# Operand steps of the down-projection issued behind named weight splits, operand sums on VectorE, and linear attention's products with v first

## The chip, the cores and the metric

One core of a Trainium2 chip runs the whole kernel. The metric is the device time in microseconds. Engines are named as in the profile: PE is TensorE (matmuls) and PEld its weight loads, DVE is VectorE, ACT is ScalarE, POOL is GpSimd, SP is SyncE, whose queue issues nearly all DMAs.

## What is computed

One decoder layer on 512 tokens of width 2048, in float32: an input projection, three groups of heads (windowed softmax attention, gated linear attention, stick-breaking attention), an output projection with a residual, and a squared-ReLU MLP with a residual, then a last RMSNorm.

```python
x = x + token_mixing(rmsnorm(x, norm_mix), w_in, ...)        # three head groups, then @ w_out
h = rmsnorm(x, norm_mlp)
x = x + jnp.square(jax.nn.relu(h @ w_mlp_in)) @ w_mlp_out     # 2048 -> 8192 -> 2048
out = rmsnorm(x, norm_final)

# inside token_mixing, linear attention in chunks of 64 tokens:
o = einsum(scores, v) + einsum(q_dec, s_prev)                 # products with v, products with the state
```

## The kernel before

**Products.** Every float32 matrix product is made of three matmuls on rounded halves: each operand x is split into hi (ScalarE rounds it to float32r) and lo (VectorE subtracts hi from x), and hi·hi, hi·lo and lo·hi are added in PSUM. The large products also use Strassen's scheme: `strassen` (L222) makes seven products A11, S1, S2, A12, S3, S4, A22 in place of eight. Their weight operands come from `t_operands` (L182): for each product it splits two halves of 128x1024 (`whi` on ScalarE at L200, `wlo` on VectorE at L201, three buffers each) and, behind the splits of each of the first four products, makes two differences of weights on VectorE (`diff`, L174).

**The up-projection** (from L1266) goes through 16 blocks b of 512 hidden columns. A block has 7 products of 2 halves of 24 matmuls each. Its results are added up and squared (`after`, `finish`) into the tiles `av`. Two blocks make one group g of 1024 columns, so there are 8 groups.

**The down-projection's operands.** Its Strassen operands (A11, A12, A22 and the sums S1 to S4 of the squared activations) are made while the up-projection runs. `down_half` (L1231) is called when a half of a block is finished. It calls `down_split` (L1223), which makes dh on ScalarE (L1226) and dl on VectorE (L1227) and issues two DMAs of 512 KB to DRAM (the tensors dS). Where S1, S2, S4 and A22 are concerned it puts closures into `later_steps`; `next_step` takes one out after each following product. dh and dl share a pool tag with two buffers, so a step that needs both waits until the two DMAs of the one before have read them.

**The down-projection** (from L1363) runs `row_group` (L944) for the 8 groups. It reads those operands back from DRAM and w_mlp_out as weights.

**Sums on GpSimd.** `mixed_operands` makes four sums of the attention output for the output projection with GpSimd in its first use (`G if k1`), and `s2_op` and `s4_op` make four sums for the first up-projection block through the table `ENG`, all on GpSimd. They are eight tensor operations of 128x1024 (L174 and L171 on POOL).

**Linear attention.** `gl_values` (L734) handles 128 tokens and four heads. For each of two pairs of heads it takes a PSUM bank and per head multiplies the scores with v (L770) and then the decayed queries with the state of each chunk (L775).

**Order.** The program is written in one order; a scheduler then orders the instructions of each engine by priority (`tc.high_priority` for weights and their splits) and by its own estimate of when they are ready. An engine's queue is in order on the chip: an instruction that waits holds all that stand behind it.

Of the kernel before, what the change touches and what calls it, by code (L numbers as in the profile page):

```python
# [10 lines left out]
F32 = mybir.dt.float32  # L11
# [4 lines left out]
ALU = mybir.AluOpType  # L16
AX = mybir.AxisListType

P = 128
# [44 lines left out]
def trunk(ctx, tc, x, norm_mix, w_in, sinks, rel_bias, gate_w, gate_b, gla_norm,  # L64
# [113 lines left out]
    ORDER0 = ("A11", "A12", "S1", "S2", "S4", "S3", "A22")  # L178

    def t_operands(quad, order, ahead=True, before=None):  # L180

# [10 lines left out]
        for p in order:  # L192
            if before:
                before(p)
            with tc.high_priority() if ahead else nullcontext():
                res = []
                for half in src[p]:
                    hi = wp.tile(shape, F32R, tag="whi", name="whi", bufs=3)
                    lo = wp.tile(shape, F32R, tag="wlo", name="wlo", bufs=3)
                    S.activation(hi, half, AF.Copy)  # L200
                    V.tensor_tensor(out=lo, in0=half, in1=hi.bitcast(F32), op=ALU.subtract)  # L201
                    res.append((hi, lo))
# [18 lines left out]

    def strassen(quad, sops, mm, nb, after, order=ORDER, before=None, by_rows=False, ahead=True):  # L222
# [511 lines left out]
    def gl_values(st, t):  # L734
# [27 lines left out]
        ssb = sm.tile([P, GLA_H], F32, tag="ssb", name="ssb")  # L762
        ob = []
        for pr, vt in enumerate(st["bv"]):
            o = pz.tile([P, 512], F32, tag="z", name="oB")
            for u in range(2):
                h = 2 * pr + u
                us = slice(u * DV, (u + 1) * DV)
                hv = slice(h * DV, (h + 1) * DV)
                T.matmul(o[:, us], lhsT=sc[:, h * P : (h + 1) * P], rhs=vt[:, us], start=(u == 0), stop=False,  # L770
                         skip_group_check=True)
                for c in range(2):
                    if prev[c] is not None:
                        cs = slice(c * 64, c * 64 + 64)
                        T.matmul(o[cs, us], lhsT=qdT[:DK, h * P + c * 64 : h * P + c * 64 + 64], rhs=prev[c][:, hv],  # L775
                                 start=False, stop=(u == 1 and c == 1), skip_group_check=True)
            for u in range(2):
                h = 2 * pr + u
# [164 lines left out]

    def row_group(acc, sops, wsrc, k1, k2, done=None, order=ORDER, rscale=None, before=None, spare=None):  # L944
        for np_ in range(2):
# [16 lines left out]
            def after(p, X, Y, Z, rows):  # L962
# [3 lines left out]
                for u in rows:  # L966
# [10 lines left out]
            strassen(quad, sops, mm, 2, after, order, None if np_ else before, by_rows=done and np_)  # L977

# [56 lines left out]
    def mixed_operands(k1, k2, tile_=lambda n: tp4.tile([P, 2, 512], F32, tag="t", name=n), spare=None):  # L1035
# [15 lines left out]

        steps = s_operands(a, put, lambda: [(spare or tile_)("spare")], (G if k1 else V,))

# [95 lines left out]

    ENG = ((G, G), (G, G))  # L1150
    STEPS = {
# [71 lines left out]
    def down_split(g, p, t, last=False):  # L1223
# [5 lines left out]
        nc.sync.dma_start(dS[g][p][1], lo.bitcast(F32))  # L1229

    def down_half(b, th):  # L1231

        g, j = divmod(b, 2)
        a = quads
        if (j, th) == (0, 0):
            down_split(g, "A11", a[1, 1])
        elif (j, th) == (0, 1):
            sub(a[1, 1], a[1, 1], a[2, 1], V)
            down_split(g, "S3", a[1, 1])
        elif (j, th) == (1, 0):  # L1240
            down_split(g, "A12", a[1, 2])
        else:
            q = dict(a)

            def s1_step():
                add(q[2, 1], q[2, 1], q[2, 2], V)
                down_split(g, "S1", q[2, 1], True)

            def s2_step():
                sub(q[1, 1], q[2, 2], q[1, 1], V)  # L1250
                down_split(g, "S2", q[1, 1])

            def s4_step():
                sub(q[1, 2], q[1, 2], q[1, 1], V)
                down_split(g, "S4", q[1, 2], True)


            later_steps.extend([lambda: down_split(g, "A22", q[2, 2]), s1_step, s2_step, s4_step])

    later_steps = []  # L1260

    def next_step():
        if later_steps:
            later_steps.pop(0)()

    for b in range(DFF // 512):  # L1266
# [44 lines left out]

        strassen(wquad, up_ops, mm, 1, after, *((ORDER0, up_operand) if b == 0 else ()), ahead=b > 0)

# [48 lines left out]
    for g in range(NG):  # L1362
# [3 lines left out]
        if g == NG - 1:  # L1366
            pool = places.pop(0)
            for nh in range(2):
                gt = slot(pool[nh], "gfin", (P, 1024))
                nc.sync.dma_start(gt, bcast(norm_final[nh * 1024 : (nh + 1) * 1024], 1024))  # L1370
                gfin.append(gt)
        row_group(acc, sops, w2, g * 1024, g * 1024 + 512,
                  *((y_done, ORDER0) if g == NG - 1 else (None, ORDER)), rscale=r2, spare=next_step)

# [32 lines left out]
```

## Time and profile before

| | us |
|---|---|
| median of 3 runs | 2130.52 (2130.04 to 2140.49) |
| the profiled execution, its own time | 2129.26 |
| its span, first to last instruction | 2127.5 |
| PE busy | 2050.9 (96%) |
| DVE busy | 1665.9 (78%) |
| ACT busy | 1038.6 (49%) |
| POOL busy | 97.8 (5%) |

The stages by the trace's clock: projections and attention up to about 690 us (linear attention about 425 to 545, windowed attention about 545 to 690, beside it the first half of the output projection), the second half of the output projection to about 800, the up-projection to about 1480, the down-projection to the end. A busy PE is not idle in the trace, but it may run at half clock: PEclk is the granted share of 2.4 GHz. A duration of one matmul overlaps that of the next; what a stretch costs PE is read from the starts.

### The profile page before, as it was taken

What the parts mean: (1) busy time and instruction counts of PE and PEld (TensorE: products, weight loads), DVE (VectorE), ACT (ScalarE), POOL (GpSimd) and SP (SyncE); (2) the same over time, 40 slices, a digit from 0 to 9 for tenths busy, and PEclk for the clock granted to TensorE, in tenths of its full rate; (3) what the DMA queues carried; (4) which work ended last, traced back from release to release, by engine and by line L of the source; (5) the groups of instructions that cost most, each with busy time, mean ns of one, the idle gap of its engine ahead of it and who ended that gap; (6) DMA issues with size and microseconds to landing.
All of it is one profiled execution on the core that took longest, in us unless ns stands there. A gap on an engine that the chain in (4) does not pass through costs nothing. (4 is left out here: it accounts for less than half of the span.)

```text
span 2127.5 us, 30668 instructions
## 1 busy us (share of the span) xinstructions
PE 2050.9 (96%) x12174; PEld 1778.3 (84%) x12174; DVE 1665.9 (78%) x1936; ACT 1038.6 (49%) x1500; POOL 97.8 (5%) x63
## 2 busy tenths in 40 slices
PE   8999999999888997999999999999999999999997
PEld 7998888777777777999999999999788888888876
DVE  7876654435787988788788788887998988888887
ACT  6436654323464555565555565564433333333334
POOL 1110000011200002000000000000000000000012
PEclk9999999999999999999999999999999999999999
DMA  6375333425534351555554464469766466455532
GB/s 221 121 159 160 118 128 109 141 98 156 192 107 155 112 175 44 181 203 187 188 216 182 167 231 179 179 235 375 259 220 236 159 215 221 178 197 218 187 130 79
DMA packets 180906, 373.17 MB, mean 175 GB/s; under 512 B 19800, under 2 KB 44186, under 8 KB 180762
## 3 DMA queue, kind: packets, MB, share of 16 engines
q1 hardware_dynamic: 180762, 371.20, 50.2%
q8 instruction: 96, 1.57, 0.3%
q14 instruction: 48, 0.39, 0.1%
HBM read 287.01 MB, written 84.15 MB: 174 GB/s over the span
## 5 line engine op out<-in xcount | busy, mean ns | idle before, releaser
L200 ACT ACTIVATE whi<-raw 128x1024 fp32r<-128x1024 f32 x532 | 561.5, 1059 | 680.9 <-PE X L960 239.0
L201 DVE TENSOR_TENSOR wlo<-raw,whi 128x1024 fp32r<-128x1024 f32 x532 | 647.8, 1229 | 150.8 <-ACT whi L200 149.2
L174 DVE TENSOR_TENSOR raw<-raw 128x1024 f32<-128x1024 f32 x304 | 370.3, 1233 | 31.3 <-DMA raw<-in_w_mlp_in 23.7
L1280 PE MATMUL X<-sh,wlo 128*128 128x256 f32 x1024 | 291.5, 285 | 11.2 <-DVE wlo L201 11.2
L1278 PE MATMUL X<-sh,whi 128*128 128x256 f32 x1024 | 290.8, 284 | 11.0 <-ACT whi L200 10.1
L1279 PE MATMUL X<-sl,whi 128*128 128x256 f32 x1024 | 289.3, 283 | 0.0
L959 PE MATMUL X<-wlo,sh 128*128 128x512 f32 x640 | 256.1, 400 | 2.9 <-DVE wlo L201 2.7
L960 PE MATMUL X<-whi,sl 128*128 128x512 f32 x640 | 254.9, 398 | 0.0
L958 PE MATMUL X<-whi,sh 128*128 128x512 f32 x640 | 232.4, 400 | 12.4 <-ACT whi L200 4.7
L1280 PEld LDWEIGHTS X<-sh,wlo 128*128 128x128 f32 x1024 | 196.3, 192 | 14.4 <-DVE wlo L201 14.4
L1278 PEld LDWEIGHTS X<-sh,whi 128*128 128x128 f32 x1024 | 196.5, 192 | 13.3 <-ACT whi L200 12.1
L1279 PEld LDWEIGHTS X<-sl,whi 128*128 128x128 f32 x1024 | 196.5, 192 | 0.0
L958 PEld LDWEIGHTS X<-whi,sh 128*128 128x128 f32 x640 | 120.5, 189 | 43.7 <-issue 6.2
L959 PEld LDWEIGHTS X<-wlo,sh 128*128 128x128 f32 x640 | 121.4, 190 | 33.9 <-DVE wlo L201 5.8
L1279 PE MATMUL Z<-sl,whi 128*128 128x256 f32 x512 | 143.3, 280 | 2.3 <-DVE sl L1108 2.3
L960 PEld LDWEIGHTS X<-whi,sl 128*128 128x128 f32 x640 | 121.3, 189 | 28.4
L1278 PE MATMUL Z<-sh,whi 128*128 128x256 f32 x512 | 143.4, 280 | 0.1
L1280 PE MATMUL Z<-sh,wlo 128*128 128x256 f32 x512 | 143.1, 280 | 0.0
L959 PE MATMUL Z<-wlo,sh 128*128 128x512 f32 x320 | 127.0, 397 | 0.5 <-DVE wlo L201 0.3
L960 PE MATMUL Z<-whi,sl 128*128 128x512 f32 x320 | 126.6, 396 | 0.0
L958 PE MATMUL Z<-whi,sh 128*128 128x512 f32 x320 | 115.3, 397 | 2.2 <-DVE acc L969 1.1
L113 DVE TENSOR_TENSOR wlo<-raw,whi 128x1024 fp32r<-128x1024 f32 x64 | 80.8, 1267 | 40.3 <-ACT whi L112 38.5
(345 smaller groups left out, 4006.1 us busy)
## 6 DMA issues: line engine op xcount, KB each, us to landing
raw<-in_w_mlp_in SPq DMA_DIRECT2D x64, 1024.0 KB, 6.0
raw<-in_w_mlp_out SPq DMA_DIRECT2D x64, 1024.0 KB, 5.9
raw<-in_w_in SPq DMA_DIRECT2D x28, 1024.0 KB, 5.0
raw<-in_w_out SPq DMA_DIRECT2D x16, 1024.0 KB, 5.2
raw<-in_w_in SPq DMA_DIRECT2D x8, 768.0 KB, 4.8
xt<-in_x SPq DMA_DIRECT2D x16, 256.0 KB, 7.4
raw<-in_w_in SPq DMA_DIRECT2D x8, 512.0 KB, 8.5
raw<-daqk SPq DMA_DIRECT2D x32, 128.0 KB, 2.7
```

Source lines behind the costliest of these rows:

```text
L113: V.tensor_tensor(out=lo, in0=part, in1=hi.bitcast(F32), op=ALU.subtract)
L174: eng.tensor_tensor(out=out_, in0=a, in1=b, op=ALU.subtract)
L200: S.activation(hi, half, AF.Copy)
L201: V.tensor_tensor(out=lo, in0=half, in1=hi.bitcast(F32), op=ALU.subtract)
L958: T.matmul(dst[u], lhsT=sh[:, kc, us], rhs=wh[:, k], start=start and k == 0, stop=False, skip_group_check=True)
L959: T.matmul(dst[u], lhsT=sh[:, kc, us], rhs=wl[:, k], start=False, stop=False, skip_group_check=True)
L960: T.matmul(dst[u], lhsT=sl[:, kc, us], rhs=wh[:, k], start=False, stop=h == 1 and k == 1, skip_group_check=True)
L1278: T.matmul(o, lhsT=wh[:, k, js], rhs=sh[:, k], start=start and j == 0 and k == 0, stop=False, skip_group_check=True)
L1279: T.matmul(o, lhsT=wh[:, k, js], rhs=sl[:, k], start=False, stop=False, skip_group_check=True)
L1280: T.matmul(o, lhsT=wl[:, k, js], rhs=sh[:, k], start=False, stop=h == 1 and k == 3, skip_group_check=True)
```

## The change

1. `later_steps` and `next_step` go. `down_half` puts every step under a key (block, product index), and `strassen` gets a function `beside`, which is called after the weight splits of each product are written and runs the steps of that key. Inside `tc.issue_after(split[0])` and `tc.issue_after(split[1])` each instruction of such a step on ScalarE is ordered behind the last `whi` split, and each on VectorE behind the last `wlo` split, of that product. These edges are an order of issue; they add no wait between engines.
2. Which step stands where changes. Product indices count from 0 in A11, S1, S2, A12, S3, S4, A22. S3 goes to index 4 of the group's second block. A22 goes to index 3, the sums S1 and S2 to index 4 and S4 to index 5 of the next block. The splits of S1 and S2 go to indices 5 and 6 of the block after that (of the next block, in the last group but one). A11 and A12 stay where they were.
3. The eight operand sums on GpSimd go to VectorE (`ENG`, `mixed_operands`).
4. In `gl_values` both PSUM banks are taken at once, all products with v come first, then those with the states, then the squares and copies.

```diff
+    split = [None, None]
@@ t_operands
-                    S.activation(hi, half, AF.Copy)
-                    V.tensor_tensor(out=lo, in0=half, in1=hi.bitcast(F32), op=ALU.subtract)
+                    split[:] = (S.activation(hi, half, AF.Copy).ins,
+                                V.tensor_tensor(out=lo, in0=half, in1=hi.bitcast(F32), op=ALU.subtract).ins)
@@ strassen
         for p, wt in t_operands(quad, order, ahead, before):
+            if beside:
+                with tc.issue_after(split[0]), tc.issue_after(split[1]):
+                    beside(order.index(p))
@@ gl_values
+        os = [pz.tile([P, 512], F32, tag="z", name="oB") for _ in range(2)]
         for pr, vt in enumerate(st["bv"]):
-            o = pz.tile([P, 512], F32, tag="z", name="oB")
+            for u in range(2):
+                h = 2 * pr + u
+                us = slice(u * DV, (u + 1) * DV)
+                T.matmul(os[pr][:, us], lhsT=sc[:, h * P : (h + 1) * P], rhs=vt[:, us], start=(u == 0), stop=False,
+                         skip_group_check=True)
+        for pr, o in enumerate(os):
             for u in range(2):
...
-                T.matmul(o[:, us], lhsT=sc[:, h * P : (h + 1) * P], rhs=vt[:, us], start=(u == 0), stop=False,
-                         skip_group_check=True)
@@ row_group, mixed_operands, table
-                if spare:
-                    spare()
-        steps = s_operands(a, put, lambda: [(spare or tile_)("spare")], (G if k1 else V,))
+        steps = s_operands(a, put, lambda: [(spare or tile_)("spare")], (V,))
-    ENG = ((G, G), (G, G))
+    ENG = ((V, V), (V, V))
@@ down_half
+        def s3():
+            sub(q[1, 1], q[1, 1], q[2, 1], V)
+            down_split(g, "S3", q[1, 1])
+        def s12():
+            add(q[2, 1], q[2, 1], q[2, 2], V)
+            sub(q[1, 1], q[2, 2], q[1, 1], V)
+        def s4():
+            sub(q[1, 2], q[1, 2], q[1, 1], V)
+            down_split(g, "S4", q[1, 2], True)
...
-            later_steps.extend([lambda: down_split(g, "A22", q[2, 2]), s1_step, s2_step, s4_step])
+            at(b + 1, 3, lambda: down_split(g, "A22", q[2, 2]))
+            at(b + 1, 4, s12)
+            at(b + 1, 5, s4)
+            then = b + 1 if g == NG - 2 else b + 2
+            at(then, 5, lambda: down_split(g, "S1", q[2, 1], True))
+            at(then, 6, lambda: down_split(g, "S2", q[1, 1]))
+    def steps_of(block):
+        def beside(i):
+            for f in steps.pop((block, i), ()):
+                f()
+        return beside
@@ up-projection, after
-            if p != "A11":
-                next_step()
```

In the rows of the order below, a name's number tells one tile from another of the same name.

VectorE where the third group ends (block 5) and block 6 begins (raw_9898 to raw_9904 are the next block's weights, av_9008, av_9009, av_9473 and av_9474 the activations of the group that ended), before:

```order
L1227 TENSOR_TENSOR dl_9835<-av_9473,dh_9834 128x1024
L201 TENSOR_TENSOR wlo_9913<-raw_9900,whi_9912 128x1024
L201 TENSOR_TENSOR wlo_9969<-raw_9898,whi_9968 128x1024
L171 TENSOR_TENSOR av_9009<-av_9009,av_9474 128x1024
L174 TENSOR_TENSOR av_9008<-av_9474,av_9008 128x1024
L174 TENSOR_TENSOR raw_9898<-raw_9902,raw_9898 128x4x256
L1227 TENSOR_TENSOR dl_10028<-av_9474,dh_10027 128x1024
L201 TENSOR_TENSOR wlo_9973<-raw_9900,whi_9972 128x1024
L174 TENSOR_TENSOR av_9473<-av_9473,av_9008 128x1024
L174 TENSOR_TENSOR raw_9898<-raw_9898 128x4x256
L201 TENSOR_TENSOR wlo_10035<-raw_9898,whi_10034 128x1024
L1227 TENSOR_TENSOR av_9009<-av_9009,dh_10093 128x1024
```

The same place after, from the same weight split on (the group's second block is now av_9455 and av_9456; av_8110 is a tile of the group before):

```order
L204 TENSOR_TENSOR wlo_9913<-raw_9900,whi_9912 128x1024
L1237 TENSOR_TENSOR dl_9829<-av_9455,dh_9828 128x1024
L204 TENSOR_TENSOR wlo_9969<-raw_9898,whi_9968 128x1024
L174 TENSOR_TENSOR raw_9898<-raw_9902,raw_9898 128x4x256
L174 TENSOR_TENSOR raw_9898<-raw_9898 128x4x256
L204 TENSOR_TENSOR wlo_9973<-raw_9900,whi_9972 128x1024
L1237 TENSOR_TENSOR dl_9843<-av_8110,dh_9842 128x1024
L174 TENSOR_TENSOR raw_9900<-raw_9904,raw_9900 128x4x256
L204 TENSOR_TENSOR wlo_10029<-raw_9898,whi_10028 128x1024
L174 TENSOR_TENSOR raw_9900<-raw_9900 128x4x256
L204 TENSOR_TENSOR wlo_10033<-raw_9900,whi_10032 128x1024
```

Of the operations on activations (av, dl) three stood between the splits wlo_9969 and wlo_9973 and three more up to the end of the piece; now one dl stands ahead of wlo_9969 and one, of the group before, behind wlo_9973; the sums come only thirteen rows behind that split.

SyncE's queue at the same place (dS are the DRAM tensors of the operands), before:

```order
L1228 DMA dS2S30_7102<-dh_9459 128x1024
L1229 DMA dS2S31_7103<-dl_9460 128x1024
L218 DMA raw_9898<-in_w_mlp_in 128x4x512
L218 DMA raw_9900<-in_w_mlp_in 128x4x512
L218 DMA raw_9902<-in_w_mlp_in 128x4x512
L218 DMA raw_9904<-in_w_mlp_in 128x4x512
L1228 DMA dS2A120_7100<-dh_9834 128x1024
```

and after:

```order
L221 DMA raw_9898<-in_w_mlp_in 128x4x512
L221 DMA raw_9900<-in_w_mlp_in 128x4x512
L1238 DMA dS2S30_7102<-dh_9707 128x1024
L1239 DMA dS2S31_7103<-dl_9708 128x1024
L1238 DMA dS1S10_7082<-dh_9772 128x1024
L221 DMA raw_9902<-in_w_mlp_in 128x4x512
L1239 DMA dS1S11_7083<-av_8111 128x1024
L221 DMA raw_9904<-in_w_mlp_in 128x4x512
```

The loads of raw_9902 and raw_9904 now stand behind the stores of S3 and of the earlier group's S1.

ScalarE in the first up-projection block (raw_7178 to raw_7184 are its weights; A22_7001 and A12_6942 are the results of the sums that were on GpSimd; sh are the rounded halves of its left operands), before:

```order
L200 ACTIVATE whi_7401<-raw_7178 128x1024
L1308 ACTIVATE av_7186<-av_7186 128x512
L1290 ACTIVATE av_7186<-av_7186 128x512
L1107 ACTIVATE sh_7397<-A22_7001 128x1024
L1305 COPY av_7187<-Z_7341 128x512
L1107 ACTIVATE sh_7468<-A12_6942 128x1024
L200 ACTIVATE whi_7405<-raw_7180 128x1024
L200 ACTIVATE whi_7472<-raw_7182 128x1024
```

and after:

```order
L203 ACTIVATE whi_7401<-raw_7178 128x1024
L1326 ACTIVATE av_7186<-av_7186 128x512
L1310 ACTIVATE av_7186<-av_7186 128x512
L203 ACTIVATE whi_7405<-raw_7180 128x1024
L203 ACTIVATE whi_7472<-raw_7182 128x1024
L1323 COPY av_7187<-Z_7341 128x512
L1117 ACTIVATE sh_7397<-A22_7001 128x1024
L203 ACTIVATE whi_7476<-raw_7184 128x1024
L1117 ACTIVATE sh_7468<-A12_6942 128x1024
```

The two weight splits whi_7405 and whi_7472, which stood behind both sh of the sums, now stand ahead of them.

## Rows read from the trace of the kernel before

**Rows 1.** The page, part 1: busy us, share of the span, number of instructions.

```profile
PE 2050.9 (96%) x12174; PEld 1778.3 (84%) x12174; DVE 1665.9 (78%) x1936; ACT 1038.6 (49%) x1500; POOL 97.8 (5%) x63
```

**Rows 2.** Waits, whole span: engine line, releaser: us in total, times, longest us.

```profile
PE X L1280 <- DVE wlo L201: 11.2, 10, 1.9
...
PE X L1278 <- ACT whi L200: 10.1, 10, 5.0
```

**Rows 3.** Timeline of PE (start, us), the same matmul in blocks 2 and 3.

```profile
927.54 0.28 PE L1278 MATMUL X<-sh,whi 128*128 128x256 f32 x1
...
966.74 0.28 PE L1278 MATMUL X<-sh,whi 128*128 128x256 f32 x1
```

**Rows 4.** Timeline of PE, second half of S2 in blocks 4, 6 and 14.

```profile
998.46 0.39 PE L1278 MATMUL X<-sh,whi 128*128 128x256 f32 x1 [0.50 <-ACT whi L200]
...
1079.73 0.39 PE L1278 MATMUL X<-sh,whi 128*128 128x256 f32 x1 [0.51 <-ACT whi L200]
...
1407.83 0.39 PE L1278 MATMUL X<-sh,whi 128*128 128x256 f32 x1 [0.52 <-ACT whi L200]
```

**Rows 5.** Windows: us, PE, PEld, DVE, ACT, POOL busy (x), PEclk, DMA, GB/s.

```profile
1066.00:1087.00 21.00, 19.18 (x145) 18.41 (x144) 21.00 (x19) 11.89 (x14) 0.00 (x0) 0.92 0.50 201
944.00:965.00 21.00, 21.00 (x183) 21.00 (x182) 18.05 (x16) 11.90 (x14) 0.00 (x0) 1.00 0.28 108
1082.00:1086.00 4.00, 3.96 (x20) 3.96 (x21) 4.00 (x4) 0.52 (x1) 0.00 (x0) 0.57 0.33 131
```

**Rows 6.** Timeline of DVE as block 6 begins, twelve operations apart.

```profile
1067.14 1.23 DVE L171 TENSOR_TENSOR av<-av 128x1024 f32<-128x1024 f32 x1
...
1080.76 3.50 DVE L201 TENSOR_TENSOR wlo<-raw,whi 128x1024 fp32r<-128x1024 f32 x3
```

**Rows 7.** DMA issues: queue, count, KB each, us from issue to landing.

```profile
dS2S<-dh SPq DMA_DIRECT2D x4, 512.0 KB, 2.6
...
dS7S<-dh SPq DMA_DIRECT2D x4, 512.0 KB, 5.6
```

**Rows 8.** Groups of instructions by line and form: busy, mean ns, idle before.

```profile
L174 POOL TENSOR_TENSOR A<-A,A 128x1024 f32<-128x1024 f32 x8 | 30.2, 3775 | 222.1 <-DVE sl L1108 145.1 <-DVE A L171 50.2 <-DVE ss L317 26.6
...
L174 DVE TENSOR_TENSOR av<-av 128x1024 f32<-128x1024 f32 x24 | 29.3, 1221 | 0.0
```

**Rows 9.** Timeline, first up-projection block: POOL, DVE, ACT and PE.

```profile
821.11 10.21 POOL L174 TENSOR_TENSOR A<-A,A 128x1024 f32<-128x1024 f32 x2 [14.28 <-DVE sl L1108]
...
804.73 3.17 DVE L1108 TENSOR_TENSOR sl<-A,sh 128x1024 fp32r<-128x1024 f32 x1
...
828.92 1.06 ACT L1107 ACTIVATE sh<-A 128x1024 fp32r<-128x1024 f32 x1 [7.76 <-POOL A L174]
...
833.40 0.58 PE L1278 MATMUL X<-sh,whi 128*128 128x256 f32 x1 [4.98 <-ACT whi L200]
```

**Rows 10.** Windows: the four us behind that PE wait, and behind another.

```profile
834.00:838.00 4.00, 2.00 (x7) 1.51 (x7) 4.00 (x5) 3.13 (x4) 0.00 (x0) 0.50 0.00 0
838.00:842.00 4.00, 4.00 (x21) 4.00 (x20) 3.48 (x4) 0.12 (x1) 0.00 (x0) 0.50 0.00 0
...
574.00:578.00 4.00, 4.00 (x16) 3.44 (x16) 2.98 (x8) 0.99 (x4) 0.00 (x0) 0.63 0.32 92
```

**Rows 11.** Timeline, windowed attention: POOL, DVE and PE.

```profile
562.26 3.14 POOL L174 TENSOR_TENSOR nat<-nat 128x1024 f32<-128x1024 f32 x1 [17.64 <-PE tp L998]
...
565.46 0.69 DVE L526 SCALAR_TENSOR_TENSOR qh<-raw,qh 64x512 fp32r<-64x512 f32 x1
...
569.47 2.71 DVE L526 SCALAR_TENSOR_TENSOR qh<-raw,qh 64x512 fp32r<-64x512 f32 x1
...
572.55 0.58 PE L539 MATMUL z<-kh,qh 128*128 128x256 f32 x1 [5.51 <-DVE oa L904]
```

**Rows 12.** Timeline of PEld, linear attention: one cycle of its two products.

```profile
481.61 0.30 PEld L770 LDWEIGHTS oB<-bva,sc 128*128 128x128 f32 x2 [0.28 <-issue]
482.13 0.20 PEld L775 LDWEIGHTS oB<-st,dT 96*64 96x64 f32 x4 [0.23 <-issue]
```

More of the change, by code (lines that the diff above doesn't have):

```diff
@@ L220, in raw_tiles, with strassen @@
         return res
-    def strassen(quad, sops, mm, nb, after, order=ORDER, before=None, by_rows=False, ahead=True):
+    def strassen(quad, sops, mm, nb, after, order=ORDER, before=None, by_rows=False, ahead=True, beside=None):
         X = Y = Z = None
         for p, wt in t_operands(quad, order, ahead, before):
+            if beside:
+                with tc.issue_after(split[0]), tc.issue_after(split[1]):
+                    beside(order.index(p))
             if p == "A11":
@@ L776, in gl_values @@
                                  start=False, stop=(u == 1 and c == 1), skip_group_check=True)
+        for pr, o in enumerate(os):
             for u in range(2):
@@ L940, in trunk, with row_group @@
     nbank[0] = -1
-    def row_group(acc, sops, wsrc, k1, k2, done=None, order=ORDER, rscale=None, before=None, spare=None):
+    def row_group(acc, sops, wsrc, k1, k2, done=None, order=ORDER, rscale=None, before=None, beside=None):
         for np_ in range(2):
@@ L971, in after @@
                         V.tensor_tensor(out=a, in0=bk[u], in1=a, op=ALU.add)
-                if spare:
-                    spare()
                 if done:
                     done(p, np_, rows)
-            strassen(quad, sops, mm, 2, after, order, None if np_ else before, by_rows=done and np_)
+            strassen(quad, sops, mm, 2, after, order, None if np_ else before, by_rows=done and np_, beside=beside)
     places = [(s1, s1, True)] * 7 + [(s1, s2, True)] + [(s2, s2, True)] * 3
@@ L1229, in down_split, with at @@
         nc.sync.dma_start(dS[g][p][1], lo.bitcast(F32))
+    steps = {}
     def down_half(b, th):
         g, j = divmod(b, 2)
-        a = quads
+        q = dict(quads)
+        def at(block, i, f):
+            steps.setdefault((block, i), []).append(f)
+        def s3():
[7 more added lines that the diff above has]
+            down_split(g, "S4", q[1, 2], True)
         if (j, th) == (0, 0):
-            down_split(g, "A11", a[1, 1])
+            down_split(g, "A11", q[1, 1])
         elif (j, th) == (0, 1):
-            sub(a[1, 1], a[1, 1], a[2, 1], V)
-            down_split(g, "S3", a[1, 1])
+            at(b + 1, 4, s3)
         elif (j, th) == (1, 0):
-            down_split(g, "A12", a[1, 2])
+            down_split(g, "A12", q[1, 2])
         else:
[L1243 to L1255, printed above, removed]
-            later_steps.extend([lambda: down_split(g, "A22", q[2, 2]), s1_step, s2_step, s4_step])
[L1260 to L1264, printed above, removed]
+            at(b + 1, 3, lambda: down_split(g, "A22", q[2, 2]))
[9 more added lines that the diff above has]
+        return beside
     for b in range(DFF // 512):
@@ L1310, in after @@
                 finish(th, nh)
-        strassen(wquad, up_ops, mm, 1, after, *((ORDER0, up_operand) if b == 0 else ()), ahead=b > 0)
+        strassen(wquad, up_ops, mm, 1, after, *((ORDER0, up_operand) if b == 0 else ()), ahead=b > 0, beside=steps_of(b))
     fsq = [sm.tile([P, 4], F32, tag="ssq4", name="fsq") for _ in range(NT)]
@@ L1371, in trunk @@
                 gfin.append(gt)
+        beside = steps_of(2 * NG + g)
         row_group(acc, sops, w2, g * 1024, g * 1024 + 512,
-                  *((y_done, ORDER0) if g == NG - 1 else (None, ORDER)), rscale=r2, spare=next_step)
+                  *((y_done, ORDER0) if g == NG - 1 else (None, ORDER)), rscale=r2, beside=beside)
 _INS = ['x', 'norm_mix', 'w_in', 'swa_sinks', 'rel_bias', 'gla_gate_w', 'gla_gate_b', 'gla_norm',
```

## The prediction, made before the changed kernel ran

> **What bounds the kernel now.** I read the page's busy times first: PE is busy 96% of the span and no other engine over 78% [rows 1], so every hole in PE's row goes straight to the end, and work on the other engines costs nothing until PE waits for it. Next, the waits, for who makes PE wait: in the up-projection it waits ten times each for the two halves of a weight split, hi from ScalarE and lo from VectorE, 21 us together [rows 2]. A wait is not the whole loss, since PE's granted clock falls afterwards, so I measure losses from starts, in the timeline. The same matmul in two blocks running starts at 927.54 and 966.74 [rows 3]: a block takes 39.20 us, and a group of two 78.40, when nothing waits. Where even blocks reach the second half of S2, the waits stand at 998.46, 1079.73 and, five groups after the first, 1407.83 [rows 4]: the first period is 81.27, and the five together 409.37 against 5 x 78.40 = 392.00. So a group boundary costs 2.87 us where it is cheapest and 17.37 / 5 = 3.47 on the mean. There are seven of them (the last seven even blocks), 7 x 3.47 = 24.3 us. The windows say why: in the 21 us ahead of such a wait VectorE is busy all 21.00, while at the boundary in the middle of a group it is busy 18.05 and PE never stops [rows 5]. Behind the wait PE's clock is granted at 0.57 for four us, 4 x 0.43 = 1.7 us of loss, which is the upper of its two levels for a small part and the lower (1.2 GHz) for the rest [rows 5]; the rest of the 3.47 is the waits themselves. VectorE's queue is therefore the limit at the seven boundaries.
>
> **The change, term A: steps at the group boundary.** Twelve operations of VectorE take 1080.76 - 1067.14 = 13.62 us when it is full [rows 6], so one of 128x1024 costs 1.135. In the order of before, from wlo_9913 to the second split of S2, six operations of the steps stand between the splits (three sums or differences of activations and three lo; five of them are in the rows shown, the last lo comes right behind): 6.8 us. After, there are two (a lo each): 2.3 us, the same count as at the boundary in the middle of a group, which does not wait. So the split comes 4.5 us earlier where it was about 2.9 us late, 1.7 to spare. The moved work is not gone, and this is where it goes: into products 3 to 6 of a block, whose weights need no differences any more. Four products are 22.4 us (7 products in 39.20). There VectorE gets eight splits (9.1), in the even block five step operations (5.7), four result additions of half the width (an estimate, half of 1.135 each: 2.3), and two differences for the next block (2.3): 19.4 of 22.4. It fits, with 3.0 us left, but the steps come in pairs: my tightest place, S4 in the even block, has about half a microsecond. On ScalarE each dh, 1.06 us (it is the same shape as the activation in [rows 9]), stands behind a split that is issued a product ahead, and adds nothing there. In SyncE's queue two weight loads now stand behind stores of S3 and S1; those loads wait for the buffers that the A22 product's splits free anyway, so I cost that at nothing; without that cover a load of 1 MB would be late by the wait of one dh, about 1 us a block. The start of the down-projection, where the last group's steps go, I cost at nothing, with 3 us either way. I take the whole 24.3 for A; its lower end is half, 12, for boundaries that stall elsewhere (first rival).
>
> **Term B: four sums of the first up-projection block.** A sum on GpSimd takes 3.78 us on the mean, the same on VectorE 1.22 [rows 8]. Four on VectorE at 1.135 add 4.5 us to its queue. The rows of the first block show what they cost now: two run from 821.11 to 831.32, ScalarE's sh waits 7.76 us for the first, the splits whi_7405 and whi_7472 stand behind it in ScalarE's queue, and PE waits 4.98 us until 833.40 [rows 9]. Then its clock stands at 0.50 for the next eight [rows 10], 4 us lost. After, both splits stand ahead of the sh; the first then waits only for its weights' difference, which I estimate at 827.0 by laying out the order with the durations of before, and with 1.06 for each split the second is done near 829.1, 4.3 us ahead of 833.40. VectorE's 4.5 more, less 1.95 that it gets back because sl is no longer stretched from 1.22 to 3.17 [rows 8, 9], takes 2.6 of that: 1.7. Upper end: 4.3 and the 4 us of half clock, 8. Lower end: nothing, or a loss of 4.5 if VectorE were the limit all through the block. I take 3, near the low end, since PE still waits there long enough to fall to the lower clock.
>
> **Term C: four sums in windowed attention.** POOL's sum starts at 562.26; beside it VectorE's qh takes 2.71 where the one before took 0.69, and PE waits 5.51 us for VectorE at 572.55 [rows 11], then runs at 0.63 for four us [rows 10], 1.5 lost. The hole and the clock are 7.0. After, one sum of 1.135 stands ahead of the chain that PE waits for, and the stretches go, 2.0 for that qh and, an estimate from it, as much again for the others. So some 3 to 4 of the hole and most of the clock: I take 5.5, with ends -4.5 (all four sums on a full VectorE) and 7.0.
>
> A rule speaks against B and C. The rows say a ratio of 3.78 to 1.22, 3.1 [rows 8]. The Trainium skill, GPSIMD Engine Reference, section "4.1 Engine selection", says that a two-input elementwise operation on GpSimd is about 2 times slower than on VectorE. By that, the eight would cost VectorE an estimated 15.1 us in place of 9.8, and B and C together would be smaller by about 5. The trace has the very operation on both engines, so the rows decide. The other rule goes the other way: SBUF — State Buffer, section "Who interferes with whom", again of the Trainium skill, has the port pair that the two engines share locked for the whole instruction. If VectorE were blocked through all 30.2 us of POOL's sums, removing them would give it 20 us net; the rows show a stretch of 2 us beside a sum of 3 [rows 11], so not all of it.
>
> **Term D: linear attention.** TensorE's weight loads sit idle 0.28 us when the shape goes from 96*64 (states) to 128*128 (v) and 0.23 when it goes back [rows 12]: 0.51 a cycle, with nothing else that ends the wait. A tile of 128 tokens has four cycles before and one after. Four tiles of four heads each: 4 x 3 x 0.51 = 6.1 us. The two banks it takes at once are of four, so I see no wait for a bank. Lower end nothing (the other work fills the gaps), upper 6.1; I take 6.1, for it is a sum over gaps in which PE did nothing.
>
> **Sum.** 24.3 + 3 + 5.5 + 6.1 = 38.9. The profiled execution took 2129.26 (span 2127.5); 2129.26 - 38.9 = 2090.4. The median of the runs lies 1.26 above the profiled one, so 2091.6, say 2092.
>
> **Rivals.** (1) The stall is moved, not removed: the steps now pile up in the even block's second half, S4 is late by more than its half microsecond (a weight load that lands late is enough), and PE waits there once a group with a fall of the clock. For it: 19.4 of 22.4 us are full. Against: the middle boundary stays without a wait at 18.05 of 21 [rows 5]. Half of A stays: 2092 + 12 = 2104. (2) The sums on VectorE give nothing: what it gets back is what it now does itself, B = C = 0: 2092 + 8.5 = 2100 or 2101. (3) All upper ends, because the holes and the clock losses go together: 24.3 + 8 + 7.0 + 6.1 = 45.4, 2085. (4) Slower: the steps now stand in fixed places of ScalarE's queue ahead of later weight splits, and dh and dl share two buffers, so a dh can wait for the store of the step before and hold the splits behind it. Three of a group's steps follow another by a product or less: 5.60 us, less 1.06 and 1.22 for dh and dl, leaves 3.3 for the store to land. The stores land in 2.6, in the last group in 5.6 [rows 7]. From 3.3 on this decides; at 5.6 in all groups each close step is 2.3 us late, 3 x 8 x 2.3 = 55 us: 2147. Against it: only one group shows 5.6. (5) The order does not hold on the chip as written and little changes: 2125 to 2135.
>
> **How the numbers follow.** The forecast as summed, 2088 to 2098: 0.48. (1) 0.20, (2) 0.10, (3) 0.14, (5) 0.04, (4) 0.04. The range goes from 2079, a little beyond (3), to 2113, which holds (1), (2) and a loss at the lower ends of B and C; it leaves out (4), (5) and tails. Half a per cent of 2130.5, 10.7 us, is about what a measurement can tell from no change: below 2119.9 counts as faster, which (1) to (3) and the forecast all are: 0.92; within 0.04, slower 0.04.
>
> **What would show it.** A: the same matmul of S2 in blocks running 39.20 us apart across group boundaries, VectorE below 20 of the 21 us there, no PE wait for whi or wlo once a group; wrong if such waits stand at another product of each group. B: PE's wait in the first block about 3 us shorter, VectorE's sl there at 1.22. C: no qh over 1 us, PE's wait under 2. D: four of the 0.51 cycles become one. The forecast falls if PE's waits for hi and lo in the up-projection still sum to over 10 us, or ScalarE's dh waits for stores for more than 3 us in several groups.

## The result and the profile after

The changed kernel takes 2100.3 us (median of 4 runs, 2099.42 to 2103.98) against 2132.1 before (2130.04 to 2140.49, 4 runs): a ratio of 0.9855, 95% interval 0.9842 to 0.9869. A second set beside later experiments gave 2097.88 against 2131.43, 0.9843 (0.9824 to 0.9861). The forecast was 2092 with a range of 2079 to 2113: right in direction and range, 8 us too hopeful. The profiled execution took 2099.42, its span 2097.6, 29.9 less than before.

The page of the changed kernel, part 1, answers to [rows 1]; the row from its part 5 and the waits of the whole span answer to [rows 2]. The lines that were L1278 to L1280 are now L1298 to L1300.

```profile
PE 2037.3 (97%) x12174; PEld 1774.7 (85%) x12174; DVE 1662.6 (79%) x1944; ACT 1036.7 (49%) x1500; POOL 70.5 (3%) x55
...
L1300 PE MATMUL X<-sh,wlo 128*128 128x256 f32 x1024 | 285.5, 280 | 1.0 <-DVE wlo L204 1.0
```

```profile
PE X L970 <- ACT whi L203: 7.3, 3, 5.1
...
PE Z L1300 <- DVE wlo L204: 3.5, 3, 2.2
...
PE X L1298 <- ACT whi L203: 2.5, 2, 1.5
...
PE X L1298 <- DVE av L1325: 2.0, 1, 2.0
```

PE's waits for weight splits in the product X of the up-projection were 11.2 and 10.1 us and are 1.0 and 2.5, all of it in block 0. The wait of L970, at the start of the down-projection, has grown (L958 before: 4.7 in all, longest 3.1), and Z of L1300 is new: 2.2 of its 3.5 stand in block 0, the rest are the two waits shown next.

A window of 21 us at the boundary into block 6, at the same distance from the block's first matmul as the first of [rows 5], and the two waits of more than 0.2 us that are left in blocks 1 to 15 (blocks are counted from 0; the texts written ahead of the runs call block 0 the first, and so on):

```profile
1047.92:1068.92 21.00, 21.00 (x183) 21.00 (x182) 18.98 (x17) 11.82 (x14) 0.00 (x0) 1.00 0.45 170
```

```profile
1196.25 0.38 PE L1300 MATMUL Z<-sh,wlo 128*128 128x256 f32 x1 [0.73 <-DVE wlo L204]
...
1353.94 0.38 PE L1300 MATMUL Z<-sh,wlo 128*128 128x256 f32 x1 [0.61 <-DVE wlo L204]
```

VectorE fell from 21.00 busy to 18.98, PE rose from 19.18 and 145 matmuls to 21.00 and 183, at full clock.

**A ledger by stage.** The starts of matmuls in PE's timeline give the length of each stage: from the 1151st matmul of the plain projections (at 418.13 before, 417.32 after) to the first of the up-projection; block 0; blocks 1 to 15, up to the start of their last matmul; from there through the first 200 matmuls of the down-projection (the transition); the rest, up to the last matmul's start. All kernels of this study, in us, from one profiled execution each (the edits are told below):

| kernel | attention, output projection | block 0 | blocks 1 to 15 | transition | rest |
|---|---|---|---|---|---|
| before | 381.6 | 63.3 | 612.4 | 53.1 | 589.3 |
| before, second profile (e0) | 383.9 | 59.8 | 613.6 | 54.3 | 592.0 |
| changed | 376.8 | 56.5 | 589.9 | 58.4 | 589.1 |
| changed, second profile (a1) | 376.1 | 56.9 | 592.9 | 57.1 | 593.5 |
| e1 steps only | 381.7 | 60.2 | 588.4 | 57.0 | 592.1 |
| e2 sums only | 378.3 | 55.8 | 612.8 | 55.0 | 590.7 |
| e3 v first only | 377.8 | 60.5 | 612.6 | 53.1 | 589.1 |
| e4 block sums only | 381.2 | 52.0 | 613.2 | 53.3 | 589.1 |
| e5 changed, no ties | 374.8 | 56.2 | 633.9 | 53.8 | 591.9 |
| e6b S3 stores on POOL's queue | 374.7 | 54.4 | 593.5 | 57.6 | 589.1 |
| e7 attention sums back | 376.7 | 53.1 | 587.9 | 57.4 | 589.1 |
| e7b the same again | 374.9 | 55.0 | 587.9 | 57.7 | 589.1 |
| e8 last S3 late | 375.5 | 55.3 | 590.7 | 56.2 | 590.6 |
| e9 last group late | 374.5 | 55.2 | 587.9 | 53.5 | 593.3 |

Read two profiles of one kernel first: they differ by 2.3 us in attention, 3.5 in block 0, 3.0 in blocks 1 to 15 and up to 4.4 in the rest. Only differences beyond that, or that several kernels repeat, count. Between before and changed the ledger says: attention 4.8 shorter, block 0 6.8, blocks 1 to 15 22.5, and the transition 5.3 longer.

### The profile page after: what moved, and what is told of

Read it like the earlier page. It is cut to its first block, busy times and chain, and to the rows that moved or that the text cites. A ratio compares the mean times of both kernels' runs of the same rounds, so it can differ in the third digit from the quotient of the medians.

```text
span 2097.6 us, 30664 instructions
## 1 busy us (share of the span) xinstructions
PE 2037.3 (97%) x12174; PEld 1774.7 (85%) x12174; DVE 1662.6 (79%) x1944; ACT 1036.7 (49%) x1500; POOL 70.5 (3%) x55
## 4 chain that ended last, share of the span: by engine, by line
PE 86%; DVE 7%; DMA 4%; ACT 1%; issue 1%; SPq 0%; POOL 0%; ACTq 0%; POOLq 0%; DVEq 0%
PE X L971 6%; PE X L972 6%; PE X L970 6%; PE acc L119 6%; PE acc L121 6%; PE acc L120 6%; PE X L1298 5%; PE X L1300 5%; PE X L1299 5%; PE Z L971 3%; PE Z L972 3%; PE Z L970 3%; PE Z L1300 3%; PE Z L1299 3%; PE Z L1298 3%; DVE raw L174 2%
## 5 line engine op out<-in xcount | busy, mean ns | idle before, releaser
L1298 PE MATMUL X<-sh,whi 128*128 128x256 f32 x1024 | 286.8, 280 | 4.5 <-ACT whi L203 2.5
L1300 PE MATMUL X<-sh,wlo 128*128 128x256 f32 x1024 | 285.5, 280 | 1.0 <-DVE wlo L204 1.0
L970 PE MATMUL X<-whi,sh 128*128 128x512 f32 x640 | 234.4, 404 | 14.6 <-ACT whi L203 7.3
L1298 PEld LDWEIGHTS X<-sh,whi 128*128 128x128 f32 x1024 | 193.7, 189 | 5.2 <-ACT whi L203 2.9
L1300 PEld LDWEIGHTS X<-sh,wlo 128*128 128x128 f32 x1024 | 193.1, 189 | 1.2 <-DVE wlo L204 1.2
L970 PEld LDWEIGHTS X<-whi,sh 128*128 128x128 f32 x640 | 121.2, 190 | 46.5 <-ACT whi L203 9.4
L1300 PE MATMUL Z<-sh,wlo 128*128 128x256 f32 x512 | 144.0, 281 | 3.5 <-DVE wlo L204 3.5
L1298 PE MATMUL Z<-sh,whi 128*128 128x256 f32 x512 | 143.6, 280 | 1.5 <-ACT av L1323 1.5
L970 PE MATMUL Z<-whi,sh 128*128 128x512 f32 x320 | 115.4, 398 | 2.1 <-DVE acc L981 1.1
```

What stands on the lines that cost most here:

```text
L970: T.matmul(dst[u], lhsT=sh[:, kc, us], rhs=wh[:, k], start=start and k == 0, stop=False, skip_group_check=True)
L1298: T.matmul(o, lhsT=wh[:, k, js], rhs=sh[:, k], start=start and j == 0 and k == 0, stop=False, skip_group_check=True)
L1300: T.matmul(o, lhsT=wl[:, k, js], rhs=sh[:, k], start=False, stop=h == 1 and k == 3, skip_group_check=True)
```

## The experiments

**Do the parts add up?** Each part alone, in the kernel before. e1 takes all of the diff but the sums and the reorder; e2:

```diff
-        steps = s_operands(a, put, lambda: [(spare or tile_)("spare")], (G if k1 else V,))
+        steps = s_operands(a, put, lambda: [(spare or tile_)("spare")], (V,))
-    ENG = ((G, G), (G, G))
+    ENG = ((V, V), (V, V))
```

e3 takes the hunk of `gl_values` alone, e4 the line `ENG` alone. e0 is the kernel before once more.

> The kernel before with the moved and tied steps alone (term A). Theory 1, the stages add up: up-projection blocks 2 to 16 give 22.5 us as in the changed kernel, and the transition to the down-projection gives 5 back, so 17 less than before, about 2113 to 2115; the PE wait at the start of the down-projection is near 5 us, not 3.1. Rival, the transition is made worse by the sums or the reorder and not by the steps: 22 less, about 2108 to 2110, the wait there near 3.1.

> The kernel before with all eight sums on VectorE and nothing else (terms B and C). Theory 1: windowed attention gives about 1, the first up-projection block 6.9, together 8, about 2122 to 2125. Rival, the prediction's sizes (3 and 5.5): the same total but 5.5 of it before 690 us. Second rival, the gain of the first block comes from the moved steps: about 1 to 3 in all, 2128 to 2131.

> The kernel before with only linear attention's reorder (term D). Theory 1, a change of shape costs PE about 0.3 us a cycle and not the 0.51 that its weight loads sit idle: 4.1 us at the end of linear attention, kept to the end, about 2126 to 2128. Rival, the prediction's 6.1: 2124 to 2126. Second rival, it is given back in windowed attention, where other waits end last: 0 to 1 at the start of the up-projection, 2130 to 2132.

> The kernel before with only the four sums of the first up-projection block on VectorE (term B). Theory 1: that block alone is 6.9 shorter (63.3 to 56.5), about 2123 to 2126. Rival, the gain there needs the attention sums to have moved too, or is the prediction's 3: 2127 to 2130.

> The kernel before, unchanged, profiled a second time. Theory: its first up-projection block, 63.3 us in the first profile, comes out at 60 to 61, as in the two variants that touch nothing in it (60.2 with the steps alone, 60.5 with the reorder alone), because one fall of the clock late in the block comes in some runs only; every other stage within half a microsecond. Rival: 63.3 again, and the 3 us belong to the edits.

Medians, each with its ratio to the runs of before in the same call: e1 2113.89, 0.9911 (0.9883 to 0.9940); e2 2122.27, 0.9943 (0.9923 to 0.9963); e3 2121.61, 0.9949 (0.9929 to 0.9968); e4 2121.07, 0.9945 (0.9924 to 0.9967). All four are gains. By medians e1, e2 and e3 give 19.3, 11.0 and 11.6, 42 together, where the whole change gives 32, and e3 and e4 lie below the times expected of them; but the intervals are 8 to 12 us wide, so the division is read from the ledger.

e1 came as expected: blocks 1 to 15 take 588.4, 24.0 less than before, and the transition 57.0, 3.9 more, with a PE wait of 5.20 there. The loss at the transition belongs to the moved steps. e0's block 0 took 59.8, just below the 60 to 61 expected, but its other stages did not stay within half a microsecond (2.3 apart in attention, 2.7 in the rest). Measured against both profiles of before, e4's block 0 (52.0) is 8 to 11 shorter, e2's (55.8) 4 to 8; the sums give that gain alone, no steps are needed. What makes the scatter between two profiles of one kernel is the fall of PE's clock, as their waits in block 0 sum to within 0.6 us of each other. The same 8 us in before and in e0 hold 58 and 69 matmuls, 1.3 us at 0.117, and the last 7 us of the block, granted 0.76 in before and 1.00 in e0, lose another 1.7:

```profile
840.00:848.00 8.00, 8.00 (x58) 8.00 (x58) 3.93 (x4) 2.67 (x4) 0.00 (x0) 0.80 0.32 99
```

```profile
840.00:848.00 8.00, 8.00 (x69) 8.00 (x68) 4.99 (x6) 3.71 (x5) 0.00 (x0) 0.97 0.38 118
```

The windows of 8 us behind the last waits of block 0, in the changed kernel and in e4:

```profile
843.00:851.00 8.00, 8.00 (x50) 8.00 (x50) 3.09 (x3) 2.03 (x4) 0.00 (x0) 0.68 0.71 281
```

```profile
848.00:856.00 8.00, 8.00 (x71) 8.00 (x70) 5.62 (x6) 4.53 (x6) 0.00 (x0) 1.00 0.74 282
```

PE was granted 0.68 in one and 1.00 in the other: 21 matmuls, 2.5 us at 0.117. Here the waits differ too: in the changed kernel PE had waited 1.03 and 2.02 us just before, in e4 1.45 once.

Against the first profile of before, e3's attention stage is 3.8 shorter, near the 4.1 expected; so is e2's, by 3.3, where 1 was expected. Together they should give 7.1 and the changed kernel shows 4.8 and 5.5. That gap alone is within the scatter, but the rows say that both remove the same hole. PE's wait of [rows 11] is in the kernels that have the sums on GpSimd and the old order of linear attention (before, e0, e1, e4: 5.51 or 5.52 each time), in e0 for instance:

```profile
571.18 0.58 PE L539 MATMUL z<-kh,qh 128*128 128x256 f32 x1 [5.52 <-DVE oa L904]
```

In e3, which still has the sums on GpSimd, it is gone, and two smaller waits stand there:

```profile
565.79 0.33 PE L878 MATMUL ptp<-ident,L 128*128 128x128 f32 x1 [1.91 <-ACT L L870]
...
570.16 0.50 PE L966 MATMUL X<-whi,sl 128*128 128x512 f32 x1 [2.00 <-DVE sl L997]
```

**Are the sums in attention worth anything, then?** e7 puts them back on GpSimd in the changed kernel (the first two lines of the diff above, reversed); e7b and a1 are e7 and the changed kernel once more, on one chip.

> The changed kernel with the four sums of the output projection's operands back on GpSimd (term C undone). Theory 1, alone the sums on VectorE gave 3.3 us before the up-projection, but together with the reorder of linear attention part is lost: 1 to 3 us slower than the changed kernel, up-projection starting at 795 to 797, 2101 to 2104. Rival, they give the 5.5 of the prediction: 2105 to 2107. Second rival, nothing or a loss: 2098 to 2100.

> Again the changed kernel with the four attention sums on GpSimd, now on the same chip as the changed kernel. Theory 1, the 5.8 us by which it was faster are falls of the clock in the first block of the one profile (3.3) and the two marginal waits of blocks 10 and 14 (2), not the sums: within 2 us of the changed kernel. Rival, the sums on VectorE do cost, through what stands behind them: 4 to 6 us faster again.

> The changed kernel, unchanged, profiled a second time beside the next three. Theory: the first up-projection block comes out between 52 and 56 and not at its 56.5, windowed attention up to 2 us shorter, because falls of the clock there come in some runs only; blocks 2 to 16 within 2 us of 22.5 gained, the transition again 5 lost: 2097 to 2101.

e7 took 2094.51 (2092.99 to 2096.25), e7b 2095.02 (2094.29 to 2102.43), ratios 0.9820 (0.9795 to 0.9845) and 0.9839 (0.9818 to 0.9859); a1 took 2097.88 (2094.13 to 2105.44). The expectation of e7 was wrong: nothing is lost. e7b's median lies 2.9 below a1's, between its two expectations, and a1's block 0 took 56.9, not the 52 to 56 expected. The attention stage with the sums on VectorE behind the new order takes 374.7 to 376.8 in five kernels (changed, a1, e5, e6b, e8) and 374.5 to 376.7 in three with them on GpSimd (e7, e7b, e9); e3, which has them there and nothing else of the change, took 377.8. So once D is made, nothing of term C shows above the scatter. In the three on GpSimd blocks 1 to 15 take 587.9, which is 15 blocks at 39.2 and no wait; in the changed kernel and in e8 waits of 1 to 3 us in all are left. Why those depend on sums made 250 us earlier was not settled.

**Is it the order or the places?** e5 keeps the new places of the steps and drops the order behind the splits.

```diff
             if beside:
-                with tc.issue_after(split[0]), tc.issue_after(split[1]):
-                    beside(order.index(p))
+                beside(order.index(p))
```

> The changed kernel with the steps at their new places in the program, but not ordered behind the weight splits. Theory 1, the order behind the splits is what keeps the steps from the group boundary, because the scheduler pulls a step forward as soon as its operands are there: half or more of the 22.5 us of the up-projection are lost again, 2112 to 2125. Rival, the new places alone do it: 2100 within 3, the blocks at 39.2.

2140.2 us (2133.67 to 2143.19, 10 runs), ratio 1.0032 (1.0017 to 1.0048): slower than before, and worse than the 2112 to 2125 expected. Blocks 1 to 15 take 633.9, 21.5 more than before and 44 more than with the ties; block 6 took 45.14. There VectorE idles for a store of the operands, and PE waits for what stands behind it. Two rows of e5's waits (some twenty of their kind) show the rest: a dh or dl whose buffer the store before has not left. In the changed kernel the largest such wait is 1.6 us, once. All such rows of ScalarE and VectorE sum to 58.5 us in e5, 24.0 in before and 5.6 in the changed kernel; so the change also took waits for stores away, which the prediction had not counted, and what part of term A they are was not separated.

```profile
1059.24 1.23 DVE L1236 TENSOR_TENSOR dl<-av,dh 128x1024 fp32r<-128x1024 f32 x1 [1.63 <-DMA dS2A<-dl]
```

```profile
ACT dh L1235 <- DMA dS1A<-dh: 4.6, 2, 3.3
...
DVE dl L1236 <- DMA dS1A<-dl: 3.0, 2, 2.5
```

```profile
1064.34 0.38 PE L1297 MATMUL X<-sh,whi 128*128 128x256 f32 x1 [1.59 <-ACT av L1322]
...
1074.24 0.39 PE L1299 MATMUL X<-sh,wlo 128*128 128x256 f32 x1 [1.13 <-DVE wlo L204]
```

So the ties carry the whole of term A. The places alone are worse than the old ones, and the rows show the mechanism of the prediction's rival (4).

**What does the transition give back?** In the changed kernel the fourth weight load of the down-projection issues 1.60 us after the last matmul of the up-projection starts (1440.49), VectorE waits for it, and PE for VectorE by way of ScalarE:

```profile
1442.09 0.38 SPq L221 DMA_DIRECT2D raw<-in_w_mlp_out  x1
```

```profile
1455.22 3.50 DVE L174 TENSOR_TENSOR raw<-raw 128x1024 f32<-128x1024 f32 x3 [1.85 <-DMA raw<-in_w_mlp_out]
```

```profile
1457.64 0.79 PE L970 MATMUL X<-whi,sh 128*128 128x512 f32 x1 [5.07 <-ACT whi L203]
```

Behind that wait PE's clock stands at 0.50 for five us (1460 to 1465).

Before, that load issued 1.40 us ahead of the last matmul's start (1475.45), and PE's wait was 3.13:

```profile
1474.05 0.38 SPq L218 DMA_DIRECT2D raw<-in_w_mlp_out  x1
```

```profile
1490.06 0.50 PE L958 MATMUL X<-whi,sh 128*128 128x512 f32 x1 [3.13 <-ACT whi L200]
```

New in SyncE's queue is the pair of stores of the last group's S3, issued 12 and 7 us ahead of the end, where before they went 33 and 32 us ahead. A pair of the group before (S2's) is new there too, 31 and 27 us ahead, where before that group's last store went 62 us ahead; no run moves that pair alone. e6b issues S3's two stores from GpSimd's queue; e8 moves the S3 step behind the transition; e9 moves every step of the last group there (those of S1 and S2 one row group on) and takes e7's edit with it.

```diff
e6b
-        nc.sync.dma_start(dS[g][p][0], hi.bitcast(F32))
-        nc.sync.dma_start(dS[g][p][1], lo.bitcast(F32))
+        q = nc.gpsimd if g == NG - 1 and p == "S3" else nc.sync
+        q.dma_start(dS[g][p][0], hi.bitcast(F32))
+        q.dma_start(dS[g][p][1], lo.bitcast(F32))
e8
-            at(b + 1, 4, s3)
+            at(*((b + 2, 3) if g == NG - 1 else (b + 1, 4)), s3)
e9 (last group only: A11, S3, A12, A22 at 3 to 6 of the first row group, sums and S4 at 4, 5 of the second)
+                at(b + 2, 3, lambda: down_split(g, "A11", q[1, 1]))
+            at(*((b + 2, 4) if g == NG - 1 else (b + 1, 4)), s3)
+                at(b + 1, 5, lambda: down_split(g, "A12", q[1, 2]))
+            at(b + 1, 6 if late else 3, lambda: down_split(g, "A22", q[2, 2]))
+            at(b + 1 + late, 4, s12)
+            at(b + 1 + late, 5, s4)
+            then = b + 1 if g == NG - 2 else b + 2 + late
```

> The changed kernel with the two stores of the last group's S3 issued from GpSimd's queue, which is idle there, in place of SyncE's. Theory 1, the two stores, now issued late, hold SyncE's queue for some 4 us ahead of the last weight loads of the down-projection's start, and PE's wait there grows from 3.1 to 5.1 with a longer fall of the clock: the transition gives back 2 to 4 us less than the 5.1, so 2096 to 2098. Rival, the loads are late for another reason (their buffers come free late, or the transfers share bandwidth): 2100 within 1, the weight load that issued at 1442.1 no earlier against the end of the up-projection.

> The changed kernel with only the last group's S3 step moved behind the transition, to index 3 of the first row group of the down-projection. Theory 2, the transition is bound by the DMA engines (busy share 1.03, some 405 GB/s, for 65 us around it in the changed kernel, 40 us in the kernel before), so its 1.05 MB of stores delay the weights by 1.05 MB / 405 GB/s = 2.6 us: the fourth weight load issues 2 to 3 us earlier against the end of the up-projection, PE's wait there goes from 5.1 to about 3, 2 to 4 us faster than the changed kernel. Theory 1 (SyncE's queue) says the same here but failed with the other queue. Rival, the order on ScalarE and VectorE makes the transition late: no change.

> A version meant to beat both kernels: the attention sums on GpSimd as in e7, and all steps of the last group (A11, S3, A12, A22, the sums, S4) moved behind the transition, to indices 3 to 6 of the first row group and 4 and 5 of the second. Theory 2: another 1.05 MB or 2.6 us of stores leave the saturated stretch, PE's wait at the transition falls below 3 and the stage loses 0 to 1 against the kernel before: 4 to 6 us faster than e7, about 2089 to 2092. Rival, the steps now make the first row groups' weight splits late: PE waits for whi or wlo of 1 us or more in the 80 us behind the transition, and the gain is gone.

e6b: 2101.47 (2098.76 to 2105.04); the fourth load still issues 1.24 us after the last matmul, PE waits 4.69. The queue is worth 0.4 us of the load's delay at most, and its theory failed. What is left are the DMA engines. Windows that begin 45 us ahead of that last matmul, of 20 us and then 40, before and changed (DMA share and GB/s are the last two columns):

```profile
1430.45:1450.45 20.00, 20.00 (x174) 20.00 (x173) 17.96 (x17) 12.65 (x15) 0.00 (x0) 1.00 0.90 310
1450.45:1490.45 40.00, 36.87 (x267) 34.26 (x265) 29.99 (x29) 19.10 (x23) 0.00 (x0) 1.00 1.03 404
```

```profile
1395.49:1415.49 20.00, 20.00 (x174) 20.00 (x173) 18.72 (x18) 13.23 (x16) 0.00 (x0) 1.00 1.02 376
1415.49:1455.49 40.00, 36.74 (x265) 33.87 (x263) 26.02 (x26) 18.40 (x22) 0.00 (x0) 1.00 1.03 405
```

In the second windows, which reach to where PE stops or stands waiting, they are busy all the time at 405 GB/s, and in the changed kernel nearly so from 45 us ahead. If that is the limit, what is stored in that stretch delays what is loaded in it, from whichever queue. e8 took 2098.69 (2093.85 to 2102.29), no faster than a1's 2097.88 where 2 to 4 us were expected, and e9 2094.03 (2092.83 to 2101.75, ratio 0.9834, 0.9812 to 0.9855), 1.0 below e7b where 4 to 6 were expected. Their fourth loads and PE's waits, e8 first (its last matmul of the up-projection starts at 1440.19, e9's at 1434.59):

```profile
1439.41 0.38 SPq L221 DMA_DIRECT2D raw<-in_w_mlp_out  x1
```

```profile
1455.40 0.80 PE L970 MATMUL X<-whi,sh 128*128 128x512 f32 x1 [3.12 <-ACT whi L203]
```

```profile
1431.41 0.38 SPq L221 DMA_DIRECT2D raw<-in_w_mlp_out  x1
```

```profile
1449.19 0.79 PE L970 MATMUL X<-whi,sh 128*128 128x512 f32 x1 [3.12 <-ACT whi L203]
```

The load issues at -0.78 in e8 and -3.18 in e9 against +1.60 (1.24 to 1.81 in the six kernels that keep the last group's steps where the change puts them): 2.4 us for each 1.05 MB of stores taken out (S3's, then A11's), where 2.6 was worked out. The two edits take the steps' work off ScalarE and VectorE too, but the last split of an up-projection weight on VectorE stands 7.1 us ahead of the end in all three (at 1433.38 in the changed kernel, 1433.09 in e8), so that work did not hold back the load's buffer. PE's wait is 3.12 in both, as in before (3.13), where VectorE does not wait for the load: the first 1.05 MB took 1.95 us off that wait, the second nothing more. The transition takes 56.2 and 53.5 where it took 57.0 to 58.4 in those six kernels. The late S3 step puts a wait of 0.98 us into e8's transition, and e9 is also rid of one of 0.34; the rest of the 2.7 between the two was not traced. e9 has the transition of before back (53.1 and 54.3) and keeps the rest. Its median is the lowest of all, but its interval overlaps that of e7b and of the changed kernel: what is shown is the transition, 4 us, not a faster kernel. Its one profile lost some 3 us to a lower clock in the last row group (granted 0.89 from 2008 to 2040, 1.00 at that place in the changed kernel), which other kernels show in some profiles too, and 0.7 to a wait in the second row group.

## Why the prediction was right, and where it was off

**A, 24.3 us, right in size and mechanism.** Alone it measured 24.0 (e1), in the changed kernel 22.5, in e7 24.5. Blocks stand at 39.20 across boundaries, and VectorE, full ahead of the boundary before, has 2 us to spare there, as the count of operations between the splits said. Rival (1) came true in small, at the product it named (S4, second half) but in odd blocks (9 and 13), where the split of the earlier group's S1 stands: 2 us, not 12.

**The transition, 0 with 3 either way: this step failed.** It cost 5.3 us between the first profiles, 4.0 between the means of two. The prediction asked of moved stores only what stands behind them in SyncE's queue, and answered that the loads wait for their buffers anyway. It did not ask how full the DMA engines were at the place where the stores went: they were at 0.90 and 310 GB/s 45 us ahead of the end and saturated from 25 us ahead, which a window of before shows. Each 1.05 MB taken out there let the next weight load issue 2.4 us earlier; PE's wait shrank by 1.95 with the first and not at all with the second.

**B, 3 us, too small.** The changed kernel gained 6.8 against the first profile of before, 3.3 against the second; e4 gained 8 to 11. The prediction let PE go on waiting behind whi_7405 and whi_7472 long enough for its clock to fall. The wait of 4.98 us is gone in both kernels (the longest left in block 0 are 2.2 and 2.5), and the clock is granted at 1.00 in the 16 us around the place (824 to 840 in the changed kernel, 830 to 846 in e4; in e7 it does fall, to 0.79 from 822 to 830), so the 4 us of half clock, left to the upper end, came too. Between the means of two profiles of each kernel the gain is 4.9.

**C, 5.5 us: wrong by double counting.** The hole it was to close is closed by the reorder too. Alone it gave 3.3; behind D nothing that shows. Each term had been worked out as if the others were not made.

**D, 6.1 us, mechanism right, size off.** One tile's products, from the first start to the next operation's start, before:

```profile
480.71 0.49 PE L770 MATMUL oB<-bva,sc 128*128 128x192 f32 x2
...
484.60 0.50 PE L120 MATMUL acc<-hT3l,whi 128*128 128x512 f32 x1
```

and after:

```profile
479.13 0.81 PE L776 MATMUL oB<-bva,sc 128*128 128x192 f32 x4
479.78 0.81 PE L776 MATMUL oB<-bvb,sc 128*128 128x192 f32 x4
480.52 1.52 PE L786 MATMUL oB<-st,dT 96*64 96x192 f32 x16
481.98 0.50 PE L121 MATMUL acc<-hT3h,wlo 128*128 128x512 f32 x1
```

3.89 us became 2.85: 1.04 a tile, 0.35 a cycle, where I had taken 0.51 from the idle time of the weight loads [rows 12]. So part of that idle time costs PE nothing. Four tiles are 4.2, and 3.8 reached the up-projection (e3).

The sum: 38.9 forecast, 29.9 between the two spans. A and the transition gave 17.2 in place of 24.3, C and D together 4.8 in place of 11.6, B 6.8 in place of 3, and the last 1 us came ahead of the ledger's start and in the rest. That the total lies only 9 us off is in part errors of opposite sign.

**The rivals and the two rules.** Rival (2) was right for C and wrong for B. Rival (4) did not happen in the changed kernel, but did in e5, when the ties were gone. On the price of a sum the prediction let the mean of 3.78 us [rows 8] decide against the rule that it had named beside it. In e7 two sums in attention take, and the same sum on VectorE in the changed kernel:

```profile
557.32 2.38 POOL L174 TENSOR_TENSOR nat<-nat 128x1024 f32<-128x1024 f32 x1 [14.83 <-PE tp L1008]
559.78 3.23 POOL L171 TENSOR_TENSOR nat<-nat 128x1024 f32<-128x1024 f32 x1
```

```profile
560.44 1.22 DVE L174 TENSOR_TENSOR nat<-nat 128x1024 f32<-128x1024 f32 x1
```

The ratio is 1.95 at best. The Trainium skill, GPSIMD Engine Reference, section "4.1 Engine selection", gives about 2, and this row agrees; the 3.1 of the mean comes from sums that ran long beside VectorE's work, up to 7.78 us for one. It changed no verdict, since the sum went by VectorE's own rows.

On the second rule, VectorE blocked through the whole of GpSimd's sums, the page of e2 decides, where the eight sums moved and nothing else:

```profile
PE 2050.9 (97%) x12174; PEld 1779.5 (84%) x12174; DVE 1664.2 (78%) x1944; ACT 1038.1 (49%) x1500; POOL 70.3 (3%) x55
```

Against [rows 1] VectorE does eight operations more, 9.8 us at 1.22, and is busy 1.7 less: it got back 11.5 of the 27.5 us by which POOL's busy time fell, not all of them, but more than the 6 that the prediction's terms B and C counted.

For term D, the Trainium skill, TensorEngine Tiling (Array Packing), section "Key Properties", says that a change of tiling mode drains TensorE; the 0.35 us for a cycle of two changes agrees with that, though no row shows the drain itself.

## What to carry to other kernels

A side step that shares an in-order engine with the critical stream should be ordered by name behind the operation that the stream needs, since new places without that order cost 44 us here. Before stores are moved, look at the DMA share and GB/s of the windows that they move into: at a share of 1.03, 1.05 MB here held the next load for 2.4 us, and another queue for them gave back 0.4. When several edits close the same hole, count it once, and judge a term of a few us by stages of two profiles, not by one.

## What was not expected of the hardware

The same matmuls ran 1% slower in some profiles at a granted clock of 1.00: 200 us of the up-projection hold 1717 matmuls of 128x256 in e9 and 1700 in e6b, without a wait in either, a block in 39.20 or 39.57.

```profile
1000.00:1200.00 200.00, 200.00 (x1717) 200.00 (x1716) 171.39 (x154) 123.69 (x147) 0.00 (x0) 1.00 0.57 203
```

```profile
1000.00:1200.00 200.00, 200.00 (x1700) 200.00 (x1699) 170.94 (x154) 122.23 (x145) 0.00 (x0) 1.00 0.56 197
```

And a fall of the clock behind waits of the same length comes in one run and not in the next, worth 3 to 4 us each in block 0 and in the last row group. Both are the scatter that the ledger shows, and neither is explained here.
